# A hybrid encoder layer: the first norm without transposes, level products in 32x32 blocks, and other places for attention's work

## The chip, the cores and the metric

The kernel runs on one core of a Trainium2 chip. The time is that of one execution on the device, in microseconds (us).

## The reference

One layer runs for two requests that share the weights: a prompt of 512 tokens and a sample of 1024, each of 1024 features, in float32.

```
h = rmsnorm(x, norm_mix_w);  proj = h @ w_in            # 1024 x 4096
q, f_fwd, f_bwd, i, g, nq, nk, nv = split(proj, 512 columns each)
o = hgrn2 forward + hgrn2 backward   # 4 heads of 128: gated linear recurrence, A(t,s) = q k decay
o_hgrn = rmsnorm(o) * gnorm_w * silu(g)
o_na = neighbourhood_attention(rmsnorm(nq), rmsnorm(nk), nv, rpb)   # 8 heads of 64, grid rows x 64
x = x + concat(o_hgrn, o_na) @ w_out
x = x + (silu(h2 @ w_gate) * (h2 @ w_up)) @ w_down,  h2 = rmsnorm(x, norm_ffn_w)
```

## The kernel before

Names: p and s are prompt and sample, hi and lo the two float32r halves into which each operand of a dense product is split; a product then takes three matmuls (hi hi, hi lo, lo hi). A "dense" matmul below is one of these, 512 columns wide.

The work is a list `units`, built at the end of `trunk` and run in order. A unit loads its weights (on the queue of SP, L108; ACT casts the high half, L109; DVE subtracts for the low half, L110), two units ahead, and issues its dense matmuls. After every few of them `quantum()` adds a rate (set by `set_mix`) to a credit, and each whole credit runs one step of a generator from a queue: the norm, a head's recurrence, attention. So the rate says how the small work lies between the dense matmuls, and `finish()` runs what is left of it without dense work between. The order on each engine is fixed in the program.

The units are, in order: p3 and p4 (columns 3 and 4 of the prompt's projection; `in_nat_unit`, which copies PSUM at L244 and writes the result to DRAM), the prompt's four heads and columns 5 to 7, the sample's columns 3, 4 and half of 5 (with the prompt's attention), the sample's heads and the rest of its columns, the prompt's output and gates (with the sample's attention), `late`, and the sample's output and feed-forward part.

The first norm (`norm_t`) loads x by tokens, sums squares on ACT (L122), makes 1/rms on DVE (L124 to L131), multiplies (L134), transposes on PE (L141, 128x128 each, four to a PSUM tile), and evicts hi on ACT (L144) and lo on DVE (L146). It runs for the prompt in unit p3, and for the sample between the dense matmuls of p3 and p4; the sample's second half goes to DRAM (hs1_d) and comes back in `load_hs1`. The constants of attention and gates (lb, rp, rpbn_d, and eighteen DMAs into bias_d on the queue of POOL) are loaded and made in the same time.

A head (`hgrn_units`) has dense products for q and two gates, then `half_mix` on 512 tokens at a time: twelve halves in all, four of them of the prompt. A half computes the matrix A of each of four chunks of 128 tokens by doubling: a base and seven levels hh = 1 to 64. Each is one group of products (`blocks`, L311) of 64x64 blocks, two by two on the diagonal of each chunk, followed by multiplications on DVE (L330 to L342) and, up to 32, a masked copy into A0 (L345); the last level copies both into A (L353). ACT makes kh (L299) ahead of each level.

## Time and profile before

| | |
|---|---|
| median of 3 runs | 1982.78 us (1982.46 to 1982.78) |
| the profiled execution | 1986.19 us, its span 1984.3 us |
| mean granted clock of TensorE | 0.993 |

The profile is of one execution. PE is TensorE's matmuls, PEld its weight loads, DVE is VectorE, ACT ScalarE, POOL GpSimd and SP SyncE, of which only the DMA queue matters here. L141 is line 141 of the kernel.  One matmul of float32 with 64 columns leaves two records, a dense one leaves one. The ends of matmuls are modelled, so distances are taken from start to start.

### The profile page before, as it was taken

The page shows a single profiled execution, that of the slowest core. Times are in us where ns is not written, and L with a number is a line of the kernel's source. Part 1 is how long each engine was busy: PE and PEld are TensorE (multiplying, and loading weights), DVE is VectorE, ACT ScalarE, POOL GpSimd, SP SyncE. Part 2 cuts the span into 40 slices and gives each one's busy share as a digit, 9 for nine tenths or more (in the row PEclk, how much of TensorE's full clock was granted, in tenths as well). Part 3 has the DMA queues.
Part 4 walks back from the last instruction along what each step waited for, and adds up shares of the span by engine and source line. Part 5 has one row for each costly group of instructions (what it writes and reads, how often), then busy time and mean ns, then how long its engine had stood idle before and what let it go on. Part 6 is the DMA issues. An engine that isn't in the chain of part 4 may idle for free.

```text
span 1984.3 us, 28394 instructions
## 1 busy us (share of the span) xinstructions
PE 1934.2 (97%) x10546; PEld 1570.9 (79%) x10546; DVE 1274.7 (64%) x2499; ACT 808.7 (41%) x1474; POOL 412.4 (21%) x416
## 2 busy tenths in 40 slices
PE   7999999999999999999999999799999999999999
PEld 5777887778778878877888888588888887888887
DVE  7687635566775757867655428976776665675643
ACT  5444434543443434655554316432333222433332
POOL 1200000000000010112122410455555452541400
PEclk9999999999999999999999999999999999999999
DMA  7823264442113137454563741232332326754443
GB/s 241 261 82 106 91 208 139 122 127 85 54 49 105 56 97 248 119 166 139 152 170 117 240 162 54 89 103 96 111 112 85 107 95 213 241 193 142 138 143 118
DMA packets 226497, 266.54 MB, mean 134 GB/s; under 512 B 19653, under 2 KB 161115, under 8 KB 226103
## 3 DMA queue, kind: packets, MB, share of 16 engines
q1 hardware_dynamic: 188448, 186.30, 31.2%
q10 hardware_dynamic: 25239, 39.63, 5.8%
q0 software_dynamic: 12672, 38.80, 5.8%
q8 instruction: 83, 1.36, 0.3%
q14 instruction: 55, 0.45, 0.1%
HBM read 194.84 MB, written 70.20 MB: 134 GB/s over the span
## 4 chain that ended last, share of the span: by engine, by line
PE 85%; DVE 7%; DMA 4%; ACT 2%; issue 1%; POOL 0%; ACTq 0%; DVEq 0%; POOLq 0%
PE pd L1041 20%; PE pm L1041 15%; PE pd L180 7%; PE pd L167 7%; PE pd L181 7%; PE pd L182 7%; PE pd L168 6%; PE pd L169 6%; PE pm L311 3%; PE pm L599 1%; PE pm L446 1%; PE pm L613 1%; PE pm L631 1%; DMA wst<-in_w_in_dram 1%; DVE w L110 1%
## 5 line engine op out<-in xcount | busy, mean ns | idle before, releaser
L110 DVE TENSOR_TENSOR w<-wst,w 128x1024 fp32r<-128x1024 f32 x128 | 157.8, 1234 | 105.5 <-ACT w L109 104.4
L109 ACT CAST w<-wst 128x1024 fp32r<-128x1024 f32 x128 | 134.1, 1049 | 168.9 <-PE pd L182 61.0
L1041 PE MATMUL pd<-bo,ao 128*128 128x512 f32 x792 | 193.9, 392 | 3.4 <-DVE bo L1036 3.4
L1041 PEld LDWEIGHTS pd<-bo,ao 128*128 128x128 f32 x792 | 149.7, 189 | 35.0 <-DVE bo L1036 3.8
L1041 PE MATMUL pm<-bo,ao 128*128 128x512 f32 x594 | 147.0, 389 | 0.0
L180 PE MATMUL pd<-h2p,w 128*128 128x512 f32 (+1 forms) x368 | 142.3, 387 | 0.6 <-ACT h2p L144 0.5
L181 PE MATMUL pd<-h2p,w 128*128 128x512 f32 (+1 forms) x368 | 140.6, 382 | 0.0
L182 PE MATMUL pd<-h2p,w 128*128 128x512 f32 (+1 forms) x368 | 140.6, 382 | 0.0
L922 POOL DMA_DIRECT2D ost<-ot_p x8 | 4.3, 540 | 649.4 <-ACT Kn L373 633.8
L167 PE MATMUL pd<-w,hs 128*128 128x512 f32 x320 | 130.6, 408 | 0.0
L1041 PEld LDWEIGHTS pm<-bo,ao 128*128 128x128 f32 x594 | 111.6, 188 | 23.2
L1041 PE MATMUL pm<-opS,w 128*128 128x512 f32 x528 | 127.0, 390 | 2.0 <-DVE sg L1214 1.4
L1041 PE MATMUL pd<-opS,w 128*128 128x512 f32 x528 | 127.0, 390 | 1.8 <-DVE u L1214 1.8
L1041 PE MATMUL pd<-opA,w 128*128 128x512 f32 x528 | 127.2, 390 | 0.0
L169 PE MATMUL pd<-w,hs 128*128 128x512 f32 x320 | 125.7, 393 | 0.0
L168 PE MATMUL pd<-w,hs 128*128 128x512 f32 x320 | 125.7, 393 | 0.0
L1041 PEld LDWEIGHTS pm<-opS,w 128*128 128x128 f32 x528 | 99.0, 188 | 23.4 <-DVE sg L1214 1.9
L1041 PEld LDWEIGHTS pd<-opS,w 128*128 128x128 f32 x528 | 99.0, 188 | 23.2 <-DVE u L1214 2.7
L1036 DVE TENSOR_TENSOR w<-wst,w 128x512 fp32r<-128x512 f32 x110 | 105.5, 976 | 15.6 <-ACT w L1035 15.2
L1041 PEld LDWEIGHTS pd<-opA,w 128*128 128x128 f32 x528 | 98.9, 188 | 20.4
L1035 ACT CAST w<-wst 128x512 fp32r<-128x512 f32 x110 | 65.0, 619 | 116.9 <-PE pd L1041 55.4
L1036 DVE TENSOR_TENSOR bo<-B,bo 128x512 fp32r<-128x512 f32 x55 | 51.9, 944 | 75.6 <-ACT bo L1035 75.4
(245 smaller groups left out, 4347.6 us busy)
## 6 DMA issues: line engine op xcount, KB each, us to landing
wst<-in_w_in_dram SPq DMA_DIRECT2D x68, 512.0 KB, 4.2
wst<-in_w_gate_dram SPq DMA_DIRECT2D x44, 512.0 KB, 4.0
wst<-in_w_up_dram SPq DMA_DIRECT2D x44, 512.0 KB, 4.1
wst<-g_S SPq DMA_DIRECT2D x44, 384.0 KB, 3.2
wst<-g_A SPq DMA_DIRECT2D x33, 384.0 KB, 3.7
g_S<-S POOLq DMA_DIRECT2D x44, 256.0 KB, 2.7
pj_s<-ev ACTq DMA_DIRECT2D x40, 256.0 KB, 2.3
bias<-bias_d SPq DMA_DIRECT2D x192, 48.0 KB, 2.9
```

The lines of the kernel that those rows point to most:

```text
L109: act.copy(out=w[:, 0, :], in_=s)
L110: dve.tensor_tensor(out=w[:, 1, :], in0=s, in1=f32(w[:, 0, :]), op=ALU.subtract)
L167: pe.matmul(ps, lhsT=xh, rhs=w[:, 0, j, :], start=k == 0, stop=False)
L168: pe.matmul(ps, lhsT=xh, rhs=w[:, 1, j, :], start=False, stop=False)
L169: pe.matmul(ps, lhsT=xl, rhs=w[:, 0, j, :], start=False, stop=k == NK - 1)
L180: pe.matmul(ps[:, ts], lhsT=wv[:, 0, k, :], rhs=xh, start=k == 0, stop=False)
L181: pe.matmul(ps[:, ts], lhsT=wv[:, 0, k, :], rhs=xl, start=False, stop=False)
L182: pe.matmul(ps[:, ts], lhsT=wv[:, 1, k, :], rhs=xh, start=False, stop=k == NK - 1)
L311: pe.matmul(ps[i * 64:i * 64 + 64, c * 64:c * 64 + 64], lhsT=lhsT[:, c * 128 + i * 64:c * 128 + i * 64 + 64], rhs=rhs(c * 128 + i * 64), s ...
L1035: act.copy(out=dst[0], in_=src)
L1036: dve.tensor_tensor(out=dst[1], in0=src, in1=f32(dst[0]), op=ALU.subtract)
L1041: pe.matmul(ps, lhsT=l[a], rhs=r[b_], start=start and i == 0, stop=stop and i == 2, skip_group_check=more)
```

## The change

The transposed inputs (xt_p, xt_s) are given beside x, and the norm's weight as a 128x8 tile nw. For the prompt, hi and lo are made from xt times nw, without 1/rms; 1/rms comes in later, as a column rs_p at the PSUM copies of `in_nat_unit` and as a row (rows_p, read from DRAM) multiplied into q and the gates. For the sample, xt is multiplied by nw and by the row of 1/rms, in half units: the first beside p3 and p4, the second in `load_hs1`, which now comes behind the opening of attention's pool. x by tokens is only loaded for the sums of squares (`stats`), the prompt's on the queue of ACT, the sample's on that of POOL. Of the levels, the base and hh up to 32 are made of 32x32 blocks, four on the diagonal of each chunk; the masked copies are 128 wide and five; A is put together by ten copies. The steps of attention's preparation for the next pair of heads (`squares`, `root`, `scaled`, `keys`, `values`, `biases`) are run at other steps k, and the rate of the sample's attention is 0.43. The part on the norm shows only its new lines.

```diff
@@ -241,14 +245,16 @@
     def in_nat_unit(b, c, hTs, groups, between):
         def done(t, ps):
             ev = pls["actB"].tile([128, 512], F32, tag="ev", bufs=2, name="ev")
-            act.copy(out=ev, in_=ps)
+            if b == "p":
+                act.activation(out=ev, in_=ps, func=AF.Copy, scale=rs_p[:, t:t + 1])
+            else:
+                act.copy(out=ev, in_=ps)
             act.dma_start(out=dram[b, c][t * 128:t * 128 + 128, :], in_=ev)
         def run(ws):
             for ts in groups:
                 if ts[0] == 4 and between is not None:
                     between()
-                need(*[(b, t) for t in ts])
                 mm_nat(hTs[b], ts, ws, done)
         return run
@@ -273,12 +279,18 @@
                 hgn["made"] += 1
                 thq = pl.tile([128, 512], F32, tag="tmp", bufs=2, name="thq")
                 g["q"] = q = pl.tile([128, 512], F32, tag="q", bufs=2, name="q")
+                if b == "p":
+                    dve.tensor_tensor(out=q, in0=ps, in1=rows["p"], op=ALU.mult)
+                    ps = q
                 act.activation(out=thq, in_=ps, func=AF.Tanh, scale=0.5)
                 dve.scalar_tensor_tensor(out=q, in0=thq, scalar=1.0, in1=ps, op0=ALU.add,
                                          op1=ALU.mult)
                 g["F"] = pl.tile([128, 2, 512], F32, tag="F", bufs=2, name="F")
                 return
             F, d = g["F"], i - 1
+            if b == "p":
+                dve.tensor_tensor(out=F[:, d, :], in0=ps, in1=rows["p"], op=ALU.mult)
+                ps = F[:, d, :]
             act.activation(out=F[:, d, :], in_=ps, func=AF.Tanh, scale=0.5)
@@ -301,31 +313,39 @@
                 return kh
             kh = khat(1)
-            A0 = pl.tile([128, 256], F32, tag="A0", bufs=2, name="A0")
-            def blocks(lhsT, rhs):
+            A0 = pl.tile([128, 128], F32, tag="A0", bufs=2, name="A0")
+            A = pl.tile([128, 4, 128], F32, tag="A", bufs=3, name="A")
+            def blocks(n, lhsT, rhs):
                 ps = mix_ps()
                 for c in range(4):
-                    for i in range(2):
-                        pe.matmul(ps[i * 64:i * 64 + 64, c * 64:c * 64 + 64],
-                                  lhsT=lhsT[:, c * 128 + i * 64:c * 128 + i * 64 + 64],
-                                  rhs=rhs(c * 128 + i * 64), start=True, stop=True)
+                    for i in range(0, 128, n):
+                        pe.matmul(ps[i:i + n, c * n:c * n + n],
+                                  lhsT=lhsT[:, c * 128 + i:c * 128 + i + n],
+                                  rhs=rhs(c * 128 + i), start=True, stop=True)
                 return ps
+            def placed(n, src, other):
+                for i in range(0, 128, n):
+                    j = i ^ n if other else i
+                    act.copy(out=A[i:i + n, :, j:j + n],
+                             in_=src[i:i + n].rearrange("p (c t) -> p c t", c=4))
             yield
-            ps = blocks(ks, lambda o: q[:, o:o + 64])
-            act.copy(out=A0, in_=ps[:, :256])
+            ps = blocks(32, ks, lambda o: q[:, o:o + 32])
+            act.copy(out=A0, in_=ps[:, :128])
             yield
             tot = F
             for li, hh in enumerate(LEVELS):
                 nb, n = 256 // hh, 512 // hh
-                if hh < 64:
-                    ps = blocks(kh, lambda o: cap(QQ, o, [[2 * hh, 32 // hh], [512 + hh, 2],
-                                                          [1, hh]]))
+                if hh < 32:
+                    ps = blocks(32, kh, lambda o: cap(QQ, o, [[2 * hh, 16 // hh], [512 + hh, 2],
+                                                              [1, hh]]))
                 else:
-                    ps = blocks(kh, lambda o: QQ[:, 1, o + 64:o + 128] if o % 128 == 0 else
-                                QQ[:, 0, o - 64:o])
+                    ps = blocks(hh, kh, lambda o: QQ[:, 1, o + hh:o + 2 * hh]
+                                if o % (2 * hh) == 0 else QQ[:, 0, o - hh:o])
                 kk = cap(KK, 0, [[512 + hh, 2], [2 * hh, nb], [1, hh]])
                 dve.tensor_tensor(out=kk, in0=kk, in1=cap(tot, 1, [[n - 1, 2], [2, nb], [0, hh]]),
                                   op=ALU.mult)
@@ -341,17 +361,14 @@
                 qf = cap(QQ, 512 + hh, [[2 * hh, nb], [1, hh]])
                 dve.tensor_tensor(out=qf, in0=qf, in1=cap(tot, 0, [[2, nb], [0, hh]]),
                                   op=ALU.mult)
-                if hh < 64:
+                if hh < 32:
                     dve.copy_predicated(out=A0.rearrange("p (c t) -> p c t", c=4),
-                                        mask=cap(mk, li * 64, [[0, 4], [1, 64]]),
-                                        data=ps[:, :256].rearrange("p (c t) -> p c t", c=4))
+                                        mask=cap(mk, li * 32, [[0, 4], [1, 32]]),
+                                        data=ps[:, :128].rearrange("p (c t) -> p c t", c=4))
                 else:
-                    A = pl.tile([128, 4, 128], F32, tag="A", bufs=3, name="A")
-                    for i in range(2):
-                        half = slice(i * 64, i * 64 + 64)
-                        for src, j in ((ps[half, :256], 1 - i), (A0[half], i)):
-                            act.copy(out=A[half, :, j * 64:j * 64 + 64],
-                                     in_=src.rearrange("p (c t) -> p c t", c=4))
+                    placed(hh, ps[:, :4 * hh], True)
+                    if hh == 32:
+                        placed(32, A0, False)
                 tot = nt
...
-            late = {}
             if H == 2:
                 if k == 0:
                     yield job(scaled, p, 1, 0)
+                    if p:
+                        yield both(job(biases, p, 1), job(values, p, 2))
                 if k == 1:
                     yield both(job(queries, p, 1), *([job(raws, q)] if q < 4 else []))
-                if k in (0, 1) and p:
-                    yield job(values, p, k + 2)
-                if k == 0 and p:
-                    yield job(biases, p, 1)
+                    if p:
+                        yield job(values, p, 3)
                 if q == 4:
                     return
                 if k == 2:
                     yield job(squares, q, 1)
+                    yield job(squares, q, 0)
                 if k == 3:
-                    yield job(squares, q, 0)
+                    yield both(job(root, q), job(scaled, q, 0, 1))
                 if k == 4:
-                    yield both(job(biases, q, 0), job(root, q), job(scaled, q, 0, 1))
+                    yield both(job(keys, q, 0), job(scaled, q, 1, 1))
+                    yield job(biases, q, 0)
                 if k == 5:
-                    yield both(job(keys, q, 0), job(scaled, q, 1, 1))
+                    yield both(job(keys, q, 1), job(scaled, q, 0, 0))
                 if k == 6:
-                    yield both(job(keys, q, 1), job(scaled, q, 0, 0), job(values, q, 0))
+                    yield both(job(queries, q, 0), job(values, q, 0))
                 if k == 7:
-                    yield both(job(queries, q, 0), job(values, q, 1))
+                    yield job(values, q, 1)
...
@@ -829,54 +846,81 @@
     stacks["n0"] = ExitStack()
     n0 = new_pool(stacks["n0"], "n0", side="right")
+    nw = cst.tile([128, NK], F32, name="nw")
+    act.dma_start(out=nw, in_=nmw)
+    rs_p = cst.tile([128, 4], F32, name="rs_p")
+    rows = {}
+    def stats(b, ts, rs, queue_):
+        n = len(ts)
+        sm = n0.tile([128, 5, n], F32, tag="sm", bufs=2, name="sm")
+        for i, t in enumerate(ts):
             x = n0.tile([128, D], F32, tag="x", bufs=4, name="x")
+            queue_.dma_start(out=x, in_=X[b][t * 128:t * 128 + 128, :])
+            yield
+            sq = n0.tile([128, D], F32, tag="sq", bufs=2, name="sq")
+            act.activation(out=sq, in_=x, func=AF.Square, accum_out=sm[:, 0, i:i + 1])
+        yield
+        rsqrt(rs, sm[:, 0, :], n, 1.0 / D, sm[:, 2:5, :])
+        yield
+    def staged(b, u, kk, pool_, tag, bufs):
+        t = pool_.tile([128, D], F32, tag=tag, bufs=bufs, name="xt")
+        ld.dma_start(out=t.rearrange("p (k t) -> p k t", k=2),
+                     in_=XT[b][kk * 256:kk * 256 + 256, u * 512:u * 512 + 512]
+                     .rearrange("(k p) t -> p k t", p=128))
+        return t.rearrange("p (k t) -> p k t", k=2)
+    def norm_p(kk):
+        if kk == 0:
+            hT["p"] = [act_tiles("hp", "actB")]
+        x = staged("p", 0, kk, n0, "xt", 4)
+        for k in (2 * kk, 2 * kk + 1):
+            hi, lo = (h[:, k, :] for h in hT["p"][0])
+            act.activation(out=hi, in_=x[:, k % 2, :], func=AF.Copy, scale=nw[:, k:k + 1])
+            dve.scalar_tensor_tensor(out=lo, in0=x[:, k % 2, :], scalar=nw[:, k:k + 1],
+                                     in1=f32(hi), op0=ALU.mult, op1=ALU.subtract)
+    def norm_rest():
+        with tc.issue_after(last["act"].ins), tc.issue_after(last["dve"].ins):
+            for _ in stats("p", range(4), rs_p, act):
+                pass
+            st.dma_start(out=rs_d["p"].rearrange("t p -> p t"), in_=rs_p)
+            constants(n0)
+    def load_rows():
+        rows["p"] = pls["hg_p"].tile([128, 512], F32, name="rows_p")
+        st.dma_start(out=rows["p"], in_=dap(rs_d["p"], 0, [[0, 128], [1, 512]]))
+    def normed(u, pool_, row, xpool, tag, bufs):
+        hT["s"][u] = act_tiles(f"hs{u}", pool_)
+        for kk in range(4):
+            x = staged("s", u, kk, xpool, tag, bufs)
+            yield
+            for k in (2 * kk, 2 * kk + 1):
+                h = x[:, k % 2, :]
+                dve.scalar_tensor_tensor(out=h, in0=h, scalar=nw[:, k:k + 1], in1=row,
+                                         op0=ALU.mult, op1=ALU.mult)
+                split([y[:, k, :] for y in hT["s"][u]], h)
+                yield
     def norm_s():
+        hT["s"] = [None, None]
+        def work():
+            rs = n0.tile([128, 8], F32, name="rs_s")
+            yield from stats("s", range(8), rs, st)
+            st.dma_start(out=rs_d["s"].rearrange("t p -> p t"), in_=rs)
+            row = n0.tile([128, 512], F32, name="row")
+            ld.dma_start(out=row, in_=dap(rs_d["s"], 0, [[0, 128], [1, 512]]))
+            yield from normed(0, "actM", row, n0, "xt", 4)
+        queue.append((always, work))
     def by_four(b):
         return [range(i, i + 4) for i in range(0, T[b] // 128, 4)]
@@ -905,9 +949,10 @@
     def load_hs1():
-        hT["s"][1] = act_tiles("hs1", "actB")
-        for i in range(2):
-            ld.dma_start(out=f32(hT["s"][1][i]), in_=hs1_d[i])
+        row = pls["na_p"].tile([128, 512], F32, name="row")
+        ld.dma_start(out=row, in_=dap(rs_d["s"], 512, [[0, 128], [1, 512]]))
+        for _ in normed(1, "actB", row, pls["na_p"], "xt", 2):
+            pass
     oT = {}
@@ -1406,15 +1451,20 @@
             r += [x, y]
         return r + a[len(b_):] + b_[len(a):]
-    units = [in_unit("p", 3, [[0], [1], [2, 3]]), in_unit("p", 4)]
-    norm_p()
-    before(units, 0, norm_s, set_mix(1.8, 2))
+    def with_x(kk, f):
+        def g():
+            norm_p(kk)
+            return f()
+        return g
+    units = [in_unit("p", 3), in_unit("p", 4)]
+    units[0][0] = [with_x(kk, f) for kk, f in enumerate(units[0][0])]
+    before(units, 0, norm_rest, norm_s, set_mix(1.8, 2))
     h, n = head_units("p"), {c: in_unit("p", c) for c in (5, 6, 7)}
     us = [h[0], h[1], n[5], h[2], h[3], n[6], n[7]]
-    units += before(us, 0, finish, close("n0"), open_pool("hg_p"), set_mix(0.75, 2))
+    units += before(us, 0, finish, close("n0"), open_pool("hg_p"), load_rows, set_mix(0.75, 2))
     h0, h1 = by_four("s")
     us = [in_unit("s", 3), in_unit("s", 4), in_unit("s", 5, [h0])]
-    units += before(us, 0, load_hs1, finish, close("hg_p"), open_pool("na_p"),
+    units += before(us, 0, finish, close("hg_p"), open_pool("na_p"), load_hs1,
                     lambda: na_jobs("p"), set_mix(0.7, 1))
     h, n = head_units("s"), {5: in_unit("s", 5, [h1]), 6: in_unit("s", 6)}
     n[7] = in_unit("s", 7, None, lambda: load_oT("p", [(0, "actM")], "actB", "ev", 2))
...
-                    set_mix(0.48, 1))
+                    set_mix(0.43, 1))
```

How the engines' orders move, at three places. On ACT, behind the first unit's casts: L863 are the squares of x (the first single one the prompt's last tile, the next five the sample's first), L249 the copies of unit p3's PSUM tiles, and L112 the first cast for unit p4. After the change:

```order
L863 ACTIVATE sq,sm<-x 128x1024
L813 DMA qkw<-in_na_k_norm_w_dram 128x64
L804 ACTIVATE lb<-lb 128x16
L818 DMA rp<-in_na_rpb_dram 120x31
L823 DMA bias_d<-neg 128x1440
L863 ACTIVATE sq,sm<-x 128x1024 x4
L249 ACTIVATE ev<-pd,rs_p 128x512
L863 ACTIVATE sq,sm<-x 128x1024
L252 DMA pj_p_87<-ev 128x512
L249 ACTIVATE ev<-pd,rs_p 128x512
L112 CAST w<-wst 128x1024
```

In the kernel before (L144 are evictions of transposes, L244 the copy of p3's first tile, L109 the casts; the constants' DMAs follow):

```order
L244 COPY ev<-pd 128x512
L109 CAST w<-wst 128x1024
L144 CAST hp_130<-pm 128x4x128
L245 DMA pj_p_87<-ev 128x512
L144 CAST hp_130<-pm 128x4x128
L779 DMA mf<-level_masks 128x384
L782 DMA lb<-in_hgrn_lb_dram 128x16x1
```

Ahead of the first cast for p4 there now stand the exponential of lb, the prompt's last square, five squares of the sample's x and two copies that need rs_p.

On POOL, whose rows are DMA issues here: x is the sample's input for the squares, rs_s the sample's 1/rms on its way to DRAM, bias_d and rpbn_d attention's biases. After the change:

```order
L860 DMA x<-in_x_sample_dram 128x1024 x4
L892 DMA rs_p<-rs_p 128x4x1
L820 DMA rpbn_d<-rp 120x31
L860 DMA x<-in_x_sample_dram 128x1024
L831 DMA bias_d<-rpbn_d 120x8x16
L831 DMA bias_d<-rpbn_d 120x16x16
L831 DMA bias_d<-rpbn_d 120x9x16
L831 DMA bias_d<-rpbn_d 120x16 x15
L860 DMA x<-in_x_sample_dram 128x1024 x3
L919 DMA rs_s<-rs_s 128x8x1
L897 DMA rows_p<-rs_p 128x512
```

In the kernel before (hs_d is the sample's second half):

```order
L803 DMA rpbn_d<-rp 120x31
L814 DMA bias_d<-rpbn_d 120x8x16
L814 DMA bias_d<-rpbn_d 120x16x16
L814 DMA bias_d<-rpbn_d 120x9x16
L814 DMA bias_d<-rpbn_d 120x16 x15
L872 DMA hs_d<-hp_544 1024x1x128
L872 DMA hs_d<-hp_545 1024x1x128
```

The sample's fifth tile of x now stands behind rpbn_d, and its last three behind the eighteen DMAs of bias_d; rs_s and the prompt's rows stand behind these.

On PE, near the end of the sample's attention: L648 are scores, L616 products with the values, L630 transposes of the softmax, L184 to L186 dense. After the change:

```order
L648 MATMUL pm<-KS,q 128x384 x4
L616 MATMUL pm<-pT,vb 64x128 x6
L184 MATMUL pd<-h2p_7999,w 128x512
L185 MATMUL pd<-h2p_8000,w 128x512
L186 MATMUL pd<-h2p_7999,w 128x512
L184 MATMUL pd<-h2p_7999,w 128x512
L185 MATMUL pd<-h2p_8000,w 128x512
L630 MATMUL pm<-ident,pr 128x128 x3
L186 MATMUL pd<-h2p_7999,w 128x512
L630 MATMUL pm<-ident,pr 128x128 x3
```

In the kernel before (L631 scores, L599 products, L613 transposes, L180 to L182 dense), from the last dense ones ahead of a step to the first behind it, of twelve between two steps:

```order
L180 MATMUL pd<-h2p_7497,w 128x512
L181 MATMUL pd<-h2p_7498,w 128x512
L182 MATMUL pd<-h2p_7497,w 128x512
L599 MATMUL pm<-pT,vb 64x128 x6
L613 MATMUL pm<-ident,pr 128x128 x6
L631 MATMUL pm<-KS,q 128x384 x4
L180 MATMUL pd<-h2p_7497,w 128x512
```

The products and the transposes stood together, with twelve dense matmuls between the scores and them; now products follow the scores at once, and five dense ones stand between the scores and the first transposes.

## Rows read from the trace of the kernel before

**Rows 1.** The page, busy time and share of the span of each engine.
```profile
PE 1934.2 (97%) x10546; PEld 1570.9 (79%) x10546; DVE 1274.7 (64%) x2499; ACT 808.7 (41%) x1474; POOL 412.4 (21%) x416
```

**Rows 2.** Windows by stage: length, busy us of each engine, clock, DMA.
```profile
0.00:75.00 75.00, 59.93 (x281) 47.04 (x282) 55.92 (x172) 42.25 (x90) 17.24 (x31) 0.98 0.81 240
258.00:400.00 142.00, 137.95 (x716) 110.01 (x715) 68.65 (x202) 67.03 (x137) 0.00 (x0) 0.99 0.50 155
```

**Rows 3.** Waits of PE by line: us in total, times, longest.
```profile
PE pm L141 <- DVE xn L134: 15.1, 5, 10.0
```

**Rows 4.** Timeline of PE in unit p3: start, us, instructions.
```profile
22.27 0.39 PE L167 MATMUL pd<-w,hp 128*128 128x512 f32 x1
22.50 0.60 PE L141 MATMUL pm<-ident,xn 128*128 128x128 f32 x4
22.85 0.48 PE L168 MATMUL pd<-w,hp 128*128 128x512 f32 x1
```

**Rows 5.** Timeline of PE at a group of level products.
```profile
108.37 0.40 PE L182 MATMUL pd<-hp,w 128*128 128x512 f32 x1
108.70 0.69 PE L311 MATMUL pm<-QQ,kh 128*64 128x64 f32 x16
109.31 0.50 PE L180 MATMUL pd<-hp,w 128*128 128x512 f32 x1
```

**Rows 6.** Timeline of PE in the prompt's attention.
```profile
295.83 0.66 PE L599 MATMUL pm<-pT,vb 128*64 128x128 f32 x8
296.42 0.66 PE L613 MATMUL pm<-ident,pr 128*128 128x128 f32 x4
```

**Rows 7.** Timeline of PE in the sample's attention.
```profile
1051.29 0.88 PE L599 MATMUL pm<-pT,vb 128*64 128x128 f32 x12
1052.10 0.88 PE L613 MATMUL pm<-ident,pr 128*128 128x128 f32 x6
1052.73 0.96 PE L631 MATMUL pm<-KS,q 128*128 128x384 f32 x4
```

**Rows 8.** Window of a head's levels, columns as in group 2.
```profile
101.00:119.00 18.00, 17.87 (x168) 13.19 (x169) 16.21 (x38) 7.52 (x14) 0.00 (x0) 1.00 0.24 73
```

**Rows 9.** Lines of DVE, 0 to 137 us: busy us, mean ns, idle before.
```profile
L134 DVE SCALAR_TENSOR_TENSOR xn<-x,nsm,wrow 128x512 f32<-128x512 f32 x24 | 17.3, 747 | 0.2
L146 DVE TENSOR_TENSOR hp<-pm,hp 128x512 fp32r<-128x512 f32 x16 | 10.4, 681 | 0.0
L130 DVE SCALAR_TENSOR_TENSOR nsm<-nsm 128x1 f32<-128x1 f32 x36 | 7.3, 215 | 0.6
```

**Rows 10.** Timeline of PE: first matmul, unit p4, head 0, first block.
```profile
13.57 0.78 PE L167 MATMUL pd<-w,hp 128*128 128x512 f32 x1
...
46.23 0.40 PE L167 MATMUL pd<-w,hp 128*128 128x512 f32 x1
...
74.95 0.39 PE L180 MATMUL pd<-hp,w 128*128 128x512 f32 x1
...
101.18 0.69 PE L311 MATMUL pm<-q,ks 128*64 128x64 f32 x16
```

**Rows 11.** DMA issues, 0 to 100 us: KB each, median us to landing.
```profile
x<-in_x_sample_dram SPq DMA_DIRECT2D x8, 512.0 KB, 4.6
lb<-in_hgrn_lb_dram ACTq DMA_DIRECT2D x1, 8.0 KB, 6.1
```

**Rows 12.** Lines of ACT, 0 to 100 us.
```profile
L122 ACT ACTIVATE xn<-x 128x512 f32<-128x512 f32 x24 | 15.0, 630 | 3.7 <-DMA x<-in_x_prompt_dram 3.7
```

**Rows 13.** Timeline of POOL's DMA issues (constants of attention).
```profile
37.67 0.68 POOL L803 DMA_DIRECT2D rpbn_d<-rp  x1 [35.13 <-DVE mx L789]
42.08 6.43 POOL L814 DMA_DIRECT2D bias_d<-rpbn_d  x9 [3.73 <-DMA rpbn_d<-rp]
...
58.12 0.53 POOL L814 DMA_DIRECT2D bias_d<-rpbn_d  x1 [0.47 <-DMA bias_d<-rpbn_d]
```

**Rows 14.** Timeline of DVE at the end of the same softmax.
```profile
1055.51 0.42 DVE L670 TENSOR_SCALAR pr<-pr,s 128x384 f32<-128x384 f32 x1
```

More of the change, by code (lines that the diff above doesn't have):

```diff
@@ L103, in act_tiles @@
                 for i in range(2)]
+    last = {}
     def load_w(src, shape):
@@ L108, in load_w @@
         ld.dma_start(out=s.rearrange("p (a b) -> p a b", a=shape[0]), in_=src)
-        act.copy(out=w[:, 0, :], in_=s)
-        dve.tensor_tensor(out=w[:, 1, :], in0=s, in1=f32(w[:, 0, :]), op=ALU.subtract)
+        last["act"] = act.copy(out=w[:, 0, :], in_=s)
+        last["dve"] = dve.tensor_tensor(out=w[:, 1, :], in0=s, in1=f32(w[:, 0, :]),
+                                        op=ALU.subtract)
         return w
@@ L729, in between @@
                 yield both(job(raws, q), job(biases, q, 0))
-                yield both(*[job(values, q, j) for j in range(4)])
+                yield both(job(squares, q, 1), *[job(values, q, j) for j in range(4)])
             if k == 1:
-                yield job(squares, q, 1)
                 yield job(squares, q, 0)
+                yield both(job(root, q), job(scaled, q, 0, 1))
             if k == 2:
-                yield both(job(root, q), job(scaled, q, 0, 1))
                 yield both(job(keys, q, 0), job(scaled, q, 0, 0))
@@ L831, in trunk @@
     n0 = new_pool(stacks["n0"], "n0", side="right")
-    wrow1 = n0.tile([128, D], F32, name="wrow1")
-    def normed(b, t, sink, after=None, lag=1):
-        def load():
-            x = n0.tile([128, D], F32, tag="x", bufs=4, name="x")
-            ld.dma_start(out=x, in_=X[b][t * 128:t * 128 + 128, :])
-            return x
-        return norm_t(load, wrow1, n0, "xn", 4, sink, after, lag)
-    def norm_p():
-        hT["p"] = [act_tiles("hp", "actB")]
-        def after(last):
-            with tc.issue_after(last.ins):
-                constants(n0)
-        for t in range(4):
-            g = normed("p", t, to_tiles(hT["p"][0], t), after if t == 3 else None)
-            norms["p", t] = g
-            next(g)
-            if t == 0:
-                act.dma_start(out=wrow1, in_=dap(nmw, 0, [[0, 128], [1, D]]))
-                next(g)
-            else:
-                queue.append((always, lambda g=g: g))
@@ L857, in norm_s @@
-    def norm_s():
-        hT["s"] = [act_tiles("hs0"), None]
-        def half1(t):
-            hh = []
-            def sink(g):
-                if g == 0:
-                    hh[:] = [n0.tile([128, NK, 128], F32R, tag=f"hp{i}", bufs=2, name=f"hp{i}")
-                             for i in range(2)]
-                return [y[:, g * 4:g * 4 + 4, :] for y in hh]
-            def after(last):
-                for i in range(2):
-                    st.dma_start(out=hs1_d[i][:, :, t * 128 - 512:t * 128 - 384], in_=f32(hh[i]))
-            return normed("s", t, sink, after, 1)
-        for t in range(8):
-            def start(t=t):
-                norms["s", t] = g = half1(t) if t >= 4 else \
-                    normed("s", t, to_tiles(hT["s"][0], t), lag=1)
-                return g
-            queue.append((always, start))
+    nw = cst.tile([128, NK], F32, name="nw")
@@ L1478, in build @@
     arrays, args = {}, []
+    inputs = dict(inputs)
+    for b in ("prompt", "sample"):
+        inputs["xt_" + b] = _np.asarray(inputs["x_" + b])[0].T
+    inputs["norm_mix_w"] = _np.asarray(inputs["norm_mix_w"])[0].reshape(NK, 128).T
     for name in _INS:
```

16 lines of the change are left out of this document (8 added, 8 removed).

## The prediction

> **What bounds the kernel now.** I read the page's busy line first [rows 1]: PE is at work for 97% of the span, so time goes only where PE has less to do or waits less. Then the windows by stage [rows 2]: in the first 75 us PE is busy for 59.9 only, while in 258 to 400 us it lacks 4; the clock is near full in both, so no term hangs on it. PE's waits by line [rows 3] say whose those first 15 us are: the norm's transposes (L141) wait for DVE's normalised x (L134).
>
> **Costs on PE.** In the dense parts one 512-wide matmul starts every 0.23 us, and a group of four transposes puts the next one off by 0.35 us (22.27 to 22.50, and 22.50 to 22.85, in [rows 4]). A block group (L311, 16 records) stands between dense matmuls that start at 108.37 and 109.31 [rows 5]: 0.94 less 0.23 is 0.71 us.
>
> **The blocks.** There are 96 such groups: base and seven levels in 12 halves. The change makes 84 of them (all but the level of 64) from eight 64x64 products into sixteen 32x32 ones: half the moving columns per product. What does their time go by? Attention's L599 also uses two column tiles, with 128 moving columns: 8 records last 0.59 us to the next row [rows 6], 12 records 0.81 [rows 7]. So two pairs more cost 0.22, one pair 0.11, and 0.59 - 0.44 = 0.15 is fixed. The L311 group's 8 pairs of 64 columns take 0.61 to the next row (108.70 to 109.31): less 0.15 that is 0.46, 0.058 a pair. Half the columns, half the time: down to 64 a pair goes by its columns. Carried on, a set of four tiles of 32 columns takes 0.03 and 8 sets 0.24 instead of 0.46: **0.2 us less in each group, -17 us in all**. At the other end a set takes no less than the pair did (0 us), because the same 128 stationary columns are loaded for it, or because each instruction has its price (16 products a group in place of 8); at over 0.06 a set it would be a loss. Nothing in the trace is narrower than 64 columns, so -17 continues a line of two points; the nearest row, L311 itself, lies on it, and I take it.
>
> The Trainium skill ("TensorE: Matmul & The Clock Gate", Back-to-back issue gap, and "TensorEngine Tiling (Array Packing)", Instruction Overhead) says that a matmul of up to some 64 moving columns takes the same (about 60 cycles), and not to take a tiling factor from a dimension that is already small. By that the groups would gain almost nothing; the row at 64 columns fits that floor and my line alike, and no run yet shows which.
>
> PE may give something back where DVE feeds the levels. In 101 to 119 us DVE is busy for 16.21 of 18 us [rows 8]; seven groups there, each 0.2 shorter, would leave 16.6. DVE loses a mask copy and half the columns of the others, but the prompt gets a 128x512 multiply by the rows for each q and gate (12 in all, some 0.68 each like L146's subtraction [rows 9]). It gets near full: **+2 us** over the twelve halves (0 if the levels interleave well, +6 if each half waits 0.5).
>
> **The start.** Gone are 96 transposes (24 groups by 0.35, 8.4 us) and the 15 us of waits for L134. From the first dense matmul at 13.57 to head 0 at 74.95 [rows 10] there are 192 dense ones, 44 of the 61 us. If nothing took the place of what is removed, PE would begin at some 8.5 us (an estimate: 5 before 13.57, for the norm ahead of the first transposes and these), be at head 0 at 52, and at the first block at 75 instead of 101.18: **-26 us at most**. But the printed orders show what takes the place. On ACT the casts of the second unit's weights (p4) now stand behind a chain: squares of the prompt's x, the constants' DMAs, the exponential of lb, the DMA of rp, squares of the sample's x up to its fifth tile, and two PSUM copies that need 1/rms. And that fifth tile's load is issued on POOL behind rpbn_d, which waits for rp. By rows: x for the statistics is asked for at 14 us (behind eight copies and four casts) and lands 4.6 later [rows 11]; three squares take 1.2 each (two of L122's halves [rows 12]), to 23; lb is issued then and lands 6.1 later [rows 11], its exponential is done at 31. rp is issued behind it and takes as long as x, so rpbn_d goes out at 36 (37.67 before [rows 13]); the fifth tile lands at 42; its square, a copy, the cast and DVE's subtraction end at 47. So unit p4 starts at 47 (46.23 before [rows 10]), though PE was done with the first unit at 31: it stands for 16 us, and ends p4 at 69.
>
> The second link is longer. The sample's last three tiles are issued behind the eighteen bias_d DMAs, which held POOL from 42.08 to 58.65 [rows 13]: now to 57. They land at 62, their squares end at 66, the small DVE chain takes 2 (ten operations of L130's 0.2 [rows 9]), the write of rs_s 4.4 (as rpbn_d, 37.67 to 42.08 [rows 13]) and its read as a row 6.1 (as lb [rows 11]): the row is there at 80 at the latest. Then DVE normalises the sample's first half, 8 products of 0.75 and 8 subtractions of 0.68 [rows 9], 11.4 us, and only behind these, in DVE's order, come the prompt's gates, and the first block some 10 us later: 102 to 107 where 101.18 was. PE has 93 dense matmuls, 21 us, for the time from 69 on, and waits for the rest. So **+4 us** (from -5, if POOL's DMAs run closer together, to +12, if each of four DMA links takes 2 us more). What is late next: the sample's own units, which begin at 258 us [rows 2] and have a first half ready by 92. Its second half is now made at their start by another 11.4 us of DVE, and PE comes to it 96 dense matmuls (22 us) later. DVE is busy for 68.7 of 142 us there [rows 2], so that costs nothing; without that cover it would be 11.
>
> **Attention.** In its last stage a step's products, transposes and scores (L599, L613, L631) came after every twelve dense matmuls. At rate 0.43 the last seven steps no longer fit ahead of the call of finish in late, and the order shows five to eight dense ones between a step's scores and its transposes. The softmax chain runs from the scores' end at 1053.69 [rows 7] to the end of L670 at 1055.93 [rows 14], 2.2 us; five dense matmuls with the next products cover 1.9, and a weight's cast or subtraction may stand between on ACT and DVE. So about 0.5 a step, **+3 us** (0 to +8). The places that moved in k = 0 to 7 trade small waits: 0, within 3 both ways. ACT has six small copies more a half, on an engine that is idle for 59% of the span [rows 1]: 0.
>
> **Sum.** +4 - 17 + 2 + 3 = -8 us. The profiled run took 1986.19 us, 1.9 more than its span, and is 3.4 above the median: 1978 by it, **1975 by the median**, which I forecast.
>
> **Rivals.**
> 1. The blocks shrink and the start goes as reckoned: the forecast, chance 0.42; its own range is 1966 to 1984.
> 2. The start gains too: POOL's queue runs faster, the row is there 15 us earlier, the first block at 92 or before. For it: a DMA issue on POOL took 0.5 to 0.7, and the eighteen spread over 16.6 by waiting for landings [rows 13]; against it, those landings are still waited for. -13 - 17 + 5 = -25: 1958. Chance 0.15.
> 3. On the other side: a set of 32 columns costs what a pair of 64 costs. Then -17 becomes 0 to -3, DVE's +2 goes, and +4 + 3 are left: +4 to +7, 1987 to 1990. It decides from about 0.05 us a set on. For it: nothing narrower than 64 was measured, and there are twice the instructions; against it, the line of [rows 5 to 7]. Chance 0.25. The skill's floor, above, would be this case.
> 4. The start is worse: the row lands ten us later, since each link waits for the one before on POOL, and the first block comes at 117. +16 - 17 + 5: 1987. Chance 0.12.
>
> The remaining 0.06 are seams of attention. A measurement of this kernel tells a change from none at about 0.2%, 4 us. Faster by more: 0.36 of case 1, 0.15, 0.03, 0.04 and 0.03, together 0.61. Same: 0.06, 0, 0.06, 0.04 and 0.01, 0.17. Slower: 0.16 of case 3, 0.04 of case 4 and 0.02, 0.22. Range: 1957 (most of case 2) to 1990 (case 3), with some 0.1 left out on each side.
>
> **What would show it.** In the changed profile: groups of L324 that put the next dense matmul off by 0.5 us (0.7 is case 3); the second unit's first matmul at 47 us, after a wait for ACT's cast or DVE's subtraction behind it; the first block at 102 to 107, and DVE busy without a gap between the row and the gates; in attention's last seven steps waits of PE for L670's successor of about 0.5 each. A first block before 95, or a set of 0.055, makes the forecast wrong.

## The result and the profile after

The changed kernel takes 2006.3 us (median of 4 runs, 2002.77 to 2009.41) where the kernel before takes 1982.78; the ratio is 1.0114, 95% interval 1.0096 to 1.0132. It is **23.5 us slower**; 1975, faster, was forecast, and 1990 was the upper end of the range. The profiled execution took 2009.41 us, its span 2007.6.

The page's first line, which answers to [rows 1]:

```profile
PE 1928.3 (96%) x11794; PEld 1547.5 (77%) x11794; DVE 1256.2 (63%) x2407; ACT 829.8 (41%) x1522; POOL 410.3 (20%) x419
```

PE's busy time fell by 6 us only, though 96 transposes are gone and 84 block groups became shorter. Its waits by line, which answer to [rows 3]:

```profile
PE pd L171 <- ACT w L112: 32.1, 2, 25.0
PE pd L184 <- ACT ev L249: 7.8, 2, 5.6
PE pm L1086 <- ACT w L1080: 7.1, 1, 7.1
PE pd L171 <- DVE x L990: 7.1, 1, 7.1
PE pm L324 <- DVE ks L307: 5.9, 1, 5.9
```

The 15.1 us of waits for L134 are gone. New in the first 120 us are 25.0 for a cast of weights ahead of unit p4 (the other 7.1 of L112's row lie ahead of the very first matmul, for which the kernel before waits 10.0), 7.8 for copies of PSUM and 5.9 ahead of the first block; a 7.1 for x (L990) is new at 1155 us. L1080's row stood before too, as 7.3.

Where the time went is seen best by the starts of the same dense matmul, counted from the first, in the traces of four kernels (worked out from the starts; us, and the difference to the kernel before; e5 and e7 are experiments below):

```
dense matmul         before    changed          e5               e7
   0  first            13.6       7.1  -6.5       7.2  -6.4       13.6   0.0
  96  unit p4          46.2      57.1 +10.9      54.1  +7.9       45.2  -1.0
 192  head 0           74.9      87.1 +12.1      88.5 +13.5       74.3  -0.7
 288  first blocks    103.5     121.7 +18.2     120.1 +16.6      100.8  -2.7
1080  attention, p    342.3     364.4 +22.1     363.8 +21.5      332.9  -9.4
2280  heads done      743.4     744.0  +0.6     742.2  -1.2      715.6 -27.8
3480  attention, s   1104.2    1098.4  -5.7    1096.9  -7.3     1073.4 -30.7
3840  output, s      1185.8    1191.0  +5.3    1188.1  +2.3     1155.5 -30.3
7217  last           1979.8    2003.4 +23.6    1983.3  +3.5     1949.6 -30.1
```

Four things stand in the changed kernel's column: 22 us lost up to the prompt's attention, 28 gained from there to the end of the sample's attention, 11 lost up to the sample's output units, and, unforeseen, 18 lost evenly over the last 3400 dense matmuls, where nothing was changed. Some 6 of the 22 and of the 28 are order alone: 46 records of attention's small matmuls, which stood behind dense matmul 1080, now stand ahead of it, and at dense matmul 1300 the difference is 13.7. In the last stage PE is busy without a gap in both traces. Its timeline at 1800 us, before and after:

```profile
1799.79 0.84 PE L1041 MATMUL pd<-bo,ao 128*128 128x512 f32 x3
1800.47 1.52 PE L1041 MATMUL pm<-bo,ao 128*128 128x512 f32 x6
1801.83 2.43 PE L1041 MATMUL pd<-bo,ao 128*128 128x512 f32 x10
```

```profile
1799.81 1.57 PE L1086 MATMUL pd<-bo,ao 128*128 128x512 f32 x6
1801.22 1.56 PE L1086 MATMUL pm<-bo,ao 128*128 128x512 f32 x6
1802.62 1.56 PE L1086 MATMUL pd<-bo,ao 128*128 128x512 f32 x6
```

From start to start, six take 1.36 us before (1800.47 to 1801.83) and 1.40 after (1801.22 to 1802.62): 0.227 and 0.234 each, by the same instructions at the same granted clock of 1.00.

The start goes the way that the prediction's chain has it, link by link later. ACT and its queue, then POOL, then DVE in the changed kernel:

```profile
30.59 5.21 ACTq L810 DMA_DIRECT2D gw<-in_hgrn_gnorm_w_dram  x1
...
38.59 0.21 ACT L804 ACTIVATE lb<-lb 128x16 f32<-128x16 f32 x1 [0.69 <-DVE lb L803]
...
54.40 1.06 ACT L863 ACTIVATE sq<-x 128x1024 f32<-128x1024 f32 x1 [9.68 <-DMA x<-in_x_sample_dram]
...
56.03 1.03 ACT L112 CAST w<-wst 128x1024 fp32r<-128x1024 f32 x1
```

```profile
43.60 0.55 POOL L820 DMA_DIRECT2D rpbn_d<-rp  x1 [1.39 <-DVE rp L819]
44.14 0.54 POOL L860 DMA_DIRECT2D x<-in_x_sample_dram  x1
52.59 6.39 POOL L831 DMA_DIRECT2D bias_d<-rpbn_d  x9 [7.91 <-DMA rpbn_d<-rp]
...
66.77 1.75 POOL L860 DMA_DIRECT2D x<-in_x_sample_dram  x3
82.15 0.91 POOL L919 DMA_DIRECT2D rs_s<-rs_s  x1 [13.63 <-DVE rs_s L99]
```

```profile
96.68 2.08 DVE L907 SCALAR_TENSOR_TENSOR xt<-xt,nw,row 128x512 f32<-128x512 f32 x3 [9.00 <-DMA row<-rs_s]
...
118.23 0.68 DVE L307 TENSOR_TENSOR ks<-KK 128x512 f32<-128x512 f32 x1
```

The exponential of lb is done at 38.8 (31 was reckoned), rpbn_d goes out at 43.6 (36), the fifth tile's square waits 9.7 us for its x and starts at 54.4 (42), and p4's first cast only then, at 56; p4 starts at 57.1 (47). The row reaches DVE at 96.7 (80), and the first block starts at 118.97 (102 to 107).

When PE goes on after its waits of 25.0, 5.6 and 5.9 us, its granted clock is 0.50, the lower of its two levels (1.2 GHz): the trace has 0.50 from 36.9 to 60.8, from 84.7 to 91.5 and from 115.4 to 125.6 us. Dense matmuls then start 0.42 to 0.43 apart, as these behind the first block:

```profile
119.55 0.80 PE L184 MATMUL pd<-hp,w 128*128 128x512 f32 x1
120.15 0.63 PE L185 MATMUL pd<-hp,w 128*128 128x512 f32 x1
120.57 0.63 PE L186 MATMUL pd<-hp,w 128*128 128x512 f32 x1
```

PE is busy for 14.7 us in these three stretches, and at 0.23 a dense matmul half of that would have done: an estimate of 7 us for the clock. In the kernel before PE is busy for 6.5 us at 0.50 up to there, in two stretches of 3.4 us, which gives 3.

A group of the levels at full clock, which answers to [rows 5]:

```profile
126.16 0.39 PE L186 MATMUL pd<-hp,w 128*128 128x512 f32 x1
126.48 0.46 PE L324 MATMUL pm<-QQ,kh 128*32 128x32 f32 x32
126.86 0.50 PE L184 MATMUL pd<-hp,w 128*128 128x512 f32 x1
```

It stands between dense starts 0.70 apart: it costs 0.47 where it cost 0.71. From its start to the next dense it takes 0.38; less the fixed 0.15 that is 0.23 for 8 sets of four records, 0.029 each (0.03 was reckoned). By the starts of the single records the sets follow each other 0.032 apart, where the pairs of 64 columns before were 0.058 apart.

### The profile page after: what moved, and what is told of

Its sections match the earlier page's. It is cut to its first block, busy times and chain, and to the rows that moved or that the text cites. A ratio compares the mean times of both kernels' runs of the same rounds, so it can differ in the third digit from the quotient of the medians.

```text
span 2007.6 us, 30832 instructions
## 1 busy us (share of the span) xinstructions
PE 1928.3 (96%) x11794; PEld 1547.5 (77%) x11794; DVE 1256.2 (63%) x2407; ACT 829.8 (41%) x1522; POOL 410.3 (20%) x419
## 4 chain that ended last, share of the span: by engine, by line
PE 82%; DMA 7%; DVE 6%; issue 2%; ACT 2%; SPq 1%; POOL 0%; ACTq 0%; DVEq 0%; POOLq 0%
PE pd L1086 20%; PE pm L1086 15%; PE pd L184 7%; PE pd L186 6%; PE pd L185 6%; PE pd L171 6%; PE pd L172 5%; PE pd L173 5%; PE pm L324 2%; DMA ost<-ot_s 2%; PE pm L616 2%; PE pm L630 2%; PE pm L648 1%; PE pm L463 1%; DMA wst<-in_w_in_dram 1%
## 5 line engine op out<-in xcount | busy, mean ns | idle before, releaser
L1086 PE MATMUL pd<-bo,ao 128*128 128x512 f32 x792 | 199.5, 398 | 3.4 <-DVE bo L1081 3.4
L112 ACT CAST w<-wst 128x1024 fp32r<-128x1024 f32 x128 | 134.2, 1049 | 139.5 <-PE pd L173 50.6
L1086 PE MATMUL pm<-bo,ao 128*128 128x512 f32 x594 | 151.8, 397 | 0.0
L184 PE MATMUL pd<-h2p,w 128*128 128x512 f32 (+1 forms) x368 | 141.7, 385 | 0.1
L186 PE MATMUL pd<-h2p,w 128*128 128x512 f32 (+1 forms) x368 | 141.1, 384 | 0.0
L1080 ACT CAST w<-wst 128x512 fp32r<-128x512 f32 x110 | 64.9, 618 | 123.4 <-PE pd L1086 59.2
```

What stands on the lines that cost most here:

```text
L112: last["act"] = act.copy(out=w[:, 0, :], in_=s)
L184: pe.matmul(ps[:, ts], lhsT=wv[:, 0, k, :], rhs=xh, start=k == 0, stop=False)
L186: pe.matmul(ps[:, ts], lhsT=wv[:, 1, k, :], rhs=xh, start=False, stop=k == NK - 1)
L1080: act.copy(out=dst[0], in_=src)
L1086: pe.matmul(ps, lhsT=l[a], rhs=r[b_], start=start and i == 0, stop=stop and i == 2, skip_group_check=more)
```

## The experiments

Every kernel below was run beside the kernel before on the same chip, whose median in these rounds was 1985.9 (e1 to e4), 1985.3 (e5 to e8), 1987.9 (e9, e10) and 1985.3 us (e11, e12); ratios are to it. For the even loss of the last stages the first theory was an address: the changed constants (mask narrower by 224 bytes a partition, nw and rs_p more by 64) move every pool of the left side by 160 bytes, those of the right side not at all.

**e1 and e2, a pad among the constants.** In the changed kernel, and in the kernel before:

```diff
     rs_p = cst.tile([128, 4], F32, name="rs_p")
+    cst.tile([128, 8], F32, name="pad")
```

```diff
     mk = cst.tile([128, 384], U8, name="mk")
+    cst.tile([128, 8], F32, name="pad")
```

> The changed kernel with 32 bytes more a partition in the pool of constants, nothing else. In the changed kernel 2826 of 7218 dense matmuls have their two operands at addresses that differ by 32 modulo 64, and these start 231 to 237 ns apart instead of 227; with the pad none differs. Theory (address phase): every dense matmul is back at 227 ns, 2826 times about 7.2 ns are gone, 20 us: about 1986 us. Rival (a slower clock or chip in that run, or the memory traffic of the late stages): the pad does nothing, 2006 us, late dense matmuls still at 231 to 237.

> The kernel before with the same 32 bytes more among its constants, which puts the same 2826 dense matmuls out of phase. Theory (address phase): about 20 us slower than before, 2003 us, the dense matmuls of the down projection at 231 to 237 ns. Rival (something else in the changed kernel slows the late stages): 1983 us.

e1: 1999.67 us, ratio 1.0074 (1.0047 to 1.0102), 6.6 less than the changed kernel and not 20. e2: 2000.36 us, ratio 1.0072 (1.0045 to 1.0098): 32 unused bytes make the kernel before 14 us slower. In its trace the last 3400 dense matmuls lose 18 us; 4 had been gained ahead of them. So addresses do matter, but modulo 64 is not the measure: e1 has all operands in phase and is slow. PE in 1800 to 1840 us (window, PE busy and matmuls, clock, DMA), e1 first, then e2:

```profile
1800.00:1840.00 40.00, 40.00 (x174) 1.00 0.44 139
```

```profile
1800.00:1840.00 40.00, 40.00 (x173) 1.00 0.43 138
```

Sorted by the distance between the two operands' addresses in a partition (the moving one's less the stationary one's), the dense matmuls' starts fall apart cleanly modulo 256. The table has those from the 3609th dense matmul on that follow each other directly, at a granted clock of 1.00 (e5 and e12 are told next):

```
kernel             distance mod 256: number, mean ns from start to start
before             0: 3561, 226.8
e3                 0: 3560, 226.8
changed            0:  782, 227.4      160: 2414, 234.2      96: 350, 233.4
e1                 0:  782, 227.7      128: 2775, 232.6
e2                 0:  783, 228.1      224: 2408, 233.4      32: 362, 233.3
e5                 0: 3545, 226.8
e12                0: 3567, 226.8
```

In the changed kernel, e1 and e2 the whole program has 4392 dense matmuls at distance 0. Both of their operands lie in pools that moved, and they stay fast: it is the distance that counts, and not where an operand lies.

**e5 and e12, the pad that keeps the distances.** e5 is e1 with a pad of 40 numbers, 160 bytes, in place of 8, which puts the left side back where it was before; e12 is e2 with 64 numbers, 256 bytes.

> The changed kernel with 160 bytes more a partition among its constants instead of the 32 of e1. In e1 the same 2826 dense matmuls stayed at 232 to 233 ns, though their operands agreed modulo 64. Over the five kernels the slow ones are those whose two operands' addresses differ modulo 256 (by 96, 128, 160 or 224); those that differ by a multiple of 256 take 227. Theory (distance modulo 256): now all are multiples, every dense matmul takes 227 again, 2826 times some 7 us/1000, 19 us below the changed kernel: 1986 to 1988. Rival (only the exact addresses of the kernel before are fast, or the run's own state): as e1, 2000, or spread.

> The kernel before with 256 bytes more among its constants (in e2 it was 32). All distances between the operands of dense matmuls stay multiples of 256, but no left-hand address is the old one. Theory (distance modulo 256): no change, dense matmuls at 227, the time within 4 us of the kernel before's in the same rounds. Rival (only the exact layout of the kernel before is fast, or any pad costs): 14 us slower, as e2.

e5: 1987.32 us, ratio 1.0008 (0.9999 to 1.0018): 19 us below the changed kernel. e12: 1985.55 us, ratio 1.0005 (0.9990 to 1.0019): no change, with the left side's addresses all moved. The same window, e5 and then e12:

```profile
1800.00:1840.00 40.00, 40.00 (x178) 1.00 0.42 136
```

```profile
1800.00:1840.00 40.00, 40.00 (x178) 1.00 0.41 134
```

178 matmuls in 40 us, where e1 and e2 had 174 and 173: shown, in both kernels, and with pads of 32, 160 and 256 bytes. Distances of 64 and 192 were not run, and what in the chip makes the distance count stays open.

**e3, the blocks alone.** The hunks on blocks, placed and A0, and the masks, in the kernel before, with a pad of 224 bytes that keeps every address:

```diff
-            ps = blocks(ks, lambda o: q[:, o:o + 64])
+            ps = blocks(32, ks, lambda o: q[:, o:o + 32])
...
-    mk = cst.tile([128, 384], U8, name="mk")
+    mk = cst.tile([128, 160], U8, name="mk")
+    cst.tile([128, 56], F32, name="pad")
```

> The kernel before with the 32x32 blocks, narrow masks and ten copies alone, and a pad that leaves all addresses of dense operands as they were. Theory (the blocks gain 0.23 us in each of 84 groups and nothing takes it back): 1983 - 20 = 1963 us. Rival (DVE bounds the levels, PE waits for it): the groups shrink as much but PE waits more, 1970 us or above.

1961.69 us, ratio 0.9878 (0.9849 to 0.9907): 24 us less by these rounds, 21 by the first rounds' 1982.78. The window that answers to [rows 8]:

```profile
101.00:119.00 18.00, 18.00 (x243) 13.49 (x242) 16.96 (x36) 11.37 (x25) 0.00 (x0) 1.00 0.25 70
```

DVE is busier, 16.96 of 18 us, and still PE has no gap: it doesn't bound the levels. The changed kernel, which has the multiplies by the rows as well, has no gap of PE from 119 to 137 us either.

**e4, the old rate in e1.**

```diff
-                    set_mix(0.43, 1))
+                    set_mix(0.48, 1))
```

> The changed kernel with the pad of e1 and the old rate 0.48 of the sample's attention. Theory (crowding): the last steps of attention no longer run among too few dense matmuls, and the heads' outputs reach DRAM early enough, so the wait of 7 us at the start of the sample's output units goes: 7 to 12 us below e1, about 1976. Rival (attention's other places are what costs, or the wait comes from the DMAs alone): within 4 us of e1, or above it, since earlier steps wait more.

1995.11 us, ratio 1.0046 (1.0031 to 1.0062): 4.6 below e1, not 7 to 12, though the wait for x at the sample's output units (7.9 in e1) is gone from its trace. From dense matmul 2520 to 3840 the changed kernel loses 4.2 us to the kernel before and e1 4.5, while e4 gains 4.7; against that, e4 came to dense matmul 2520 4.3 later than e1. The same edit gave 7.5 from e6 to e8 and 8.7 from e9 to e10.

**e7, blocks and places in the kernel before.** e3 with the whole hunk on the function between, at rate 0.48.

> e3 (the kernel before with the 32x32 blocks, addresses kept) with attention's other places as well, at the old rate 0.48. Theory (the places gain at this rate): 5 us below e3, about 1957. Rival (they gain only in the changed kernel, whose heads are shorter, or trade waits): within 3 us of e3, 1960 to 1964.

1956.96 us, ratio 0.9856 (0.9839 to 0.9872): 4.7 below e3, and **the fastest version of all**, 28 us below the kernel before in the same rounds. e3 ran in other rounds on another chip, and the intervals of the two ratios overlap; but in the traces e3 loses 1.9 us to the kernel before from dense matmul 2520 to 3840 and e7 gains 2.5, so the places' gain, 4.4, lies where they are.

**e6, e8, e9, e10 and e11, the start put in another order**, all with e5's pad. e6 takes the bias constants out of `constants`, behind the sample's norm in the code, and reads rows_p on ACT's queue (the line that moves them):

```diff
             yield from normed(0, "actM", row, n0, "xt", 4)
+            bias_constants(n0)
```

e9 starts the sample's norm a unit later, and loads the prompt's x on POOL's queue with no wait for the first unit's casts; e8 and e10 are e6 and e9 at rate 0.48, and e11 is e10 with `constants` out of that wait too. Of e9's edit, the lines on the unit are:

```diff
-    before(units, 0, norm_rest, norm_s, set_mix(1.8, 2))
+    before(units, 0, norm_rest)
+    before(units, 1, norm_s, set_mix(1.8, 2))
```

> e5 with attention's bias constants taken out of the gates' constants: rp no longer waits behind the squares on ACT, and the eighteen bias DMAs no longer stand on POOL between the sample's fifth tile and its last three (the order puts them ahead of all of them); the prompt's rows are read on ACT's queue. Theory (the order of these DMAs is what makes the statistics late): the row arrives 15 to 25 us earlier, the first block at 95 to 105 us instead of 118, and the time is 12 to 20 us below e5: about 1970. Rival (memory traffic or the squares on ACT set the start): within 5 us of e5.

> e6 with the rate 0.48 as in e4. Theory (the late end of attention costs 4 to 7 us, the start's order some 15): 1965, above e7 by what is left of the start and of making the second half of hs on DVE, some 5 to 10 us. Rival (the norm without transposes is better once its DMAs are in order): below e7.

> e6 showed that the row came 16 us earlier and the first block still not, since the casts of unit p4's weights stood on ACT behind all eight squares of the sample, and p4 began 13 us later than in e5. Here the sample's statistics are begun at unit p4 instead of p3, so that p4's weights are cast first, and the prompt's x for the squares is loaded from the start, on POOL's queue, so that rs_p, for which p3's PSUM copies wait, is there before p3's dense matmuls end. Theory (the start is bound by what stands ahead of those casts and copies on ACT, not by traffic): p4 begins by 40 us instead of 54, the first block comes at 90 to 100 us instead of 118, the time is 15 to 28 us below e5: 1960 to 1972. Rival (DMA traffic of the first 40 us is the bound, 14 MB in all): p4 begins after 48, the time is within 6 us of e5.

> e9 with the rate 0.48. Theory: 5 to 8 us below e9, as e4 to e1 and e8 to e6; 1955 to 1965, so about e7. Rival (the changed norm, well ordered, gains more than its transposes cost): clearly below e7's 1957.

> e10 with the gates' small constants asked for at the very start, ahead of the bulk, instead of at 21 us, where lb took 20 us to land among other DMAs and its exponential held ACT's casts and copies until 42.6. Theory (one thing after another stands on ACT ahead of p4's casts and p3's copies): p4 begins at 36 to 42 us instead of 47.5, the first block at 95 to 108 instead of 117, 1962 to 1972. Rival (the DMAs' traffic of 14 MB in the first 40 us is the bound whatever the order): p4 later than 46, within 4 us of e10, 1978.

```
                 median us, ratio to before              p4    head 0   first block
before           (1982.8)                               46.2     74.9    101.2
e5               1987.32  1.0008 (0.9999 to 1.0018)     54.1     88.5    117.4
e6               1996.09  1.0044 (1.0030 to 1.0057)     66.7    103.4    125.7
e8 (e6, 0.48)    1988.59  1.0007 (0.9997 to 1.0016)     67.0    104.2    126.5
e9               1986.42  0.9991 (0.9981 to 1.0000)     48.6     92.4    116.0
e10 (e9, 0.48)   1977.76  0.9949 (0.9932 to 0.9965)     47.5     91.8    115.9
e11              1976.41  0.9962 (0.9950 to 0.9973)     51.9     93.3    116.6
```

The expected starts failed each time, and by the same pattern: what was moved came earlier, and the next thing on ACT stood in its place. In e6 all eight squares came to stand ahead of p4's casts. In e9 the casts wait behind lb again, which was 20.4 us on its way among the bulk (ACT's timeline):

```profile
42.63 0.21 ACT L804 ACTIVATE lb<-lb 128x16 f32<-128x16 f32 x1 [12.70 <-DVE lb L803]
```

In e11 lb is early, but gw's issue now holds ACT from 2.3 to 13.9 us, so that the first hi copies come at 14.0 and the first matmul at 17.4; the row is at DVE at 89.1, 1.2 sooner than in e9. The windows of e11, columns as in [rows 2], suggest why an order alone wins little:

```profile
0.00:20.00 20.00, 1.22 (x2) 0.50 (x2) 3.14 (x8) 6.86 (x11) 3.50 (x12) 1.00 0.90 296
20.00:40.00 20.00, 19.84 (x76) 16.17 (x77) 11.97 (x31) 12.95 (x20) 3.40 (x6) 1.00 0.87 294
40.00:60.00 20.00, 11.39 (x36) 8.36 (x35) 3.06 (x3) 9.18 (x16) 2.91 (x4) 0.74 0.79 205
```

The DMA engines are busy for 0.87 to 0.90 of the first 40 us: xt has to come as well as x. Whether traffic is the bound by itself stays open (no run took the loads away).

## Why the prediction was wrong

**The sum's silent step.** "In the dense parts one 512-wide matmul starts every 0.23 us" was taken for a constant of 7218 matmuls. It became 0.234 for those whose operands' distance changed, 2826 by the program's addresses. This was in no term and in no rival, and it is 19 us (the changed kernel less e5; 21 by the two ratios), most of the 23.5. It hung on three lines that look like bookkeeping: nw, rs_p and the tile of the masks, mk. With e5's pad the change is no measurable difference.

**The start: the mechanism was right, the size was not.** The step is "So +4 us": it measured +18.2 at the 288th dense matmul. The chain named was the one that ran, but the landings of [rows 11] were used as if they were fixed. By DMA issues of the changed kernel the sample's tiles took a median of 7.0 us to land, the prompt's 8.0, and gw's issue held ACT's queue for 5.21 us, so the chain ran later and later: by 8 us at lb's exponential, 12 at the fifth tile's square, 17 at the row. Rival 4 (first block at 117, +16) is what happened, at 118.97; it had a chance of 0.12. e5, where the addresses are as before, has its price too, 1987, but there is luck in that: the blocks gained more than rival 4 has for them, and other small losses took it back.

**The clock.** "The clock is near full in both, so no term hangs on it" was read from the kernel before, whose longest wait of PE up to there is 10 us. The prediction itself reckoned with a wait of 16 us ahead of p4, which became 25.0. Behind the new waits the granted clock was 0.50; by the busy times above that is at most some 4 us more than before, up to 126 us.

**The cover of the second half.** "So that costs nothing" was nearly right. By the table of starts the changed kernel loses another 4 us between 288 and 1080, but the order of attention's steps is in that. From dense matmul 288 to 1300, where both kernels have done the same small matmuls, the kernel before takes 314.4 us, e3 (the blocks alone) 305.6 and the changed kernel 309.9: 4.3 more than e3. Some 2.0 of these are the clock up to 125.6 us (3.9 us of PE at 0.50), and PE's waits are 4.8 in place of e3's 3.1, among them 1.3 for L249's copy.

**The blocks: right.** -17 was the term; 0.24 a group on PE is 20, and e3 alone gave 24 by its rounds, 21 by the first. The line through 128 and 64 columns goes on to 32. The Trainium skill ("TensorE: Matmul & The Clock Gate", Back-to-back issue gap) gives a matmul of 1 to 64 columns one time, about 60 cycles, and by that rival 3 would have held. For these float32 products the trace disagrees: a set of 32 columns starts 0.032 us after the set before it, a pair of 64 started 0.058 after the pair before it. At the granted clock of 1.00 (2.4 GHz) these are some 76 and 140 cycles, so the row at 64 columns did not fit that floor, though the prediction says that it does; what is narrower than 32 columns was not run. The +2 for DVE was not there: neither e3's window nor the changed kernel's has a gap.

**Attention: right in size, by two parts that cancel.** +3 was forecast and 4.2 measured over that stage. The places, held for 0, gain 4.4 to 4.7 (e7 less e3), and the rate costs 4.6 to 8.7 by the times, 9 by the starts of that stage in e1 and e4; that +3 came out was luck. The loss was not in the last seven steps, where PE hardly waits; it is in the wait of 7.1 us at the sample's output units, which goes with the rate (e4). There the outputs of attention come back from DRAM one load after another, and ACT and DVE split them, up to the moment at which PE goes on. The prediction asked for the start "what is late next", and did not ask it here.

**What the norm is worth.** e10 has the new norm in about the best order that was tried, the blocks, the places, the old rate and kept distances: 1977.8. e7 has all that with the old norm: 1957.0. So the norm without transposes costs 18 (by the ratios, since the two ran on different chips) to 21 us in the orders that were tried, where the transposes that it removes were 8.4 us of PE and 15 of waits.

## What to carry to other kernels

A change in the size of a tile can move all tiles allocated behind it, as it did here: compare the operands' distances in the program before and after, and look at the spacing of untouched matmuls in a late stage first, since a small loss in each of thousands outweighs a stall of 15 us. A wait that is removed at the start is worth only what the next chain leaves of it: list what stands ahead, on each in-order engine and queue, of the first instruction that must be early, and price its DMAs by a busy stretch, not by a median. Small products gained by their columns down to 32, so cutting work that is thrown away paid at once.

## What the runs showed of the hardware

A 128x128 by 512 float32r matmul that follows another takes 226.8 ns from start to start when the addresses of its two operands differ by a multiple of 256 bytes (before, e3, e5, e12), and 233.3, 233.4, 232.6, 234.2 and 233.4 when they differ by 32, 96, 128, 160 and 224 modulo 256 (e2, changed, e1, changed, e2), at a granted clock of 1.00 in all of them. Four column tiles of 32 columns, with 32 moving ones in float32, take 0.032 us from one set of four records to the next, and a product leaves two records; two column tiles of 64 with 64 moving columns take 0.058. Behind PE's waits of 5.6 to 25.0 us in the changed kernel the granted clock was 0.50, and dense matmuls started 0.42 to 0.43 us apart.
